# Down projection of a SwiGLU block as seven block products in place of eight, with casts and block sums moved between engines

## The chip, the cores and the metric

One NeuronCore of one Trainium2 chip runs the whole program. The metric is device microseconds for one execution; a kernel's time is the median of several. Six names are used for what works in parallel: TensorE (PE, matmuls; PEld are its loads of the standing operand), VectorE (DVE), ScalarE (ACT), GpSimd (POOL), the 16 DMA engines, and SyncE (SP), whose queue issues nearly all transfers here.

## The reference, cut to what matters

One layer of a latent backbone over 2048 tokens of width 1024. Attention, a gated scan and a Fourier mix come first and are not touched. What the change is about is the end:

```python
x_new = x + g1 * y
x_new = x_new + g2 * swiglu_ffn(modulate(x_new, norm2_g[l], sh2, sc2), w_gate_up[l], w_down[l])
return rms_norm(x_new, final_norm_g)

def swiglu_ffn(h, w_gu, w_dn):
    gate, up = jnp.split(h @ w_gu, 2, axis=-1)
    return (jax.nn.silu(gate) * up) @ w_dn
```

`w_gate_up` is 1024 x 5632 and `w_down` 2816 x 1024, all in float32.

## The kernel before

Every float32 product is made of three matmuls in a 32-bit reduced format (fp32r): an operand `a` is split into a high part (a cast, `hi`) and a low part (`a` minus its cast, `lo`, always on VectorE), and `mm3` adds high x low, high x high and low x high into one PSUM bank. So each operand tile of 128 x 512 costs one cast and one subtraction. The casts of weights (`wparts`) run on GpSimd, those of activations (`split`) on ScalarE.

**Gate-up.** A Strassen-like scheme of seven block products is in use already. The 2048 tokens are two halves `s` of 1024, each two blocks of 512; one unit `(s, j)` works out 128 gate and 128 up features for one half. Its seven products (order 6, 1, 7, 5, 2, 3, 4; 12 matmuls each, 84 a unit, 44 units) gather in three banks, named x, y and z, that are read between products: `act.copy(e6, acc)` after 6, `act.copy(e, acc)` after 1, adds on VectorE after 7, 5, 3 and 4, the gate's SiLU on ScalarE. A bank goes on to its next product when that read is done. Between the products the seven weight operands of the next unit are summed (`left_sums`) and split (`wparts`). The unit's results, `e` and `f`, are the hidden activations of two token blocks; they are stored to DRAM (`hid[b]`). At `s` = 1 new token operands are loaded and split in the last unit of the first half.

**Down.** For each of 4 blocks of 512 tokens and each half of the 1024 output columns, four banks (one per tile of 128 tokens) gather over the 22 tiles of 128 hidden features, in groups of four: `rows` calls `mm3` for every tile. Weights come in pieces of 1024 KB (`wd`, four tiles) and are split for every block anew; hidden tiles are loaded and split once for both column halves. Behind each bank `final` multiplies by the gate `g2`, adds the residual row (`xnew`, loaded again), squares for the norm, and after the second half scales the row tile and stores it: VectorE (L1379, L1380), ScalarE (L1382), GpSimd (L1386, L1387: the power -0.5), then VectorE (L1391) for one half, and ScalarE (L1393) and GpSimd (L1394) for the other.

**Order.** The program is written as one sequence. A planner at build puts each engine's and each queue's instructions into an order, from the written one, the dependencies and its own estimates of durations; an instruction waits on semaphores, and an engine works through its queue in that order. Tiles come from pools with a number of buffers per tag (`wp`: 9 split weights; `h6`, `h1`: 4 each; `wr`: 2 raw pieces); who asks for a buffer waits for the last reader of its old contents.

## Time and profile before

| | us |
|---|---|
| median of 3 runs | 3324.02 |
| lowest, highest | 3322.12, 3328.81 |
| the profiled execution | 3332.05 |
| its span, first to last instruction | 3330.3 |
| TensorE busy in it | 3166.0 |

The rows further down come from the profiled execution, which took 8.0 us more than the median; their times count from the start of its span. Gate-up ends and down begins at 2837.9 us. A row gives an engine's line in the program, the operation, what is written and what is read, and times; a matmul's duration is pipelined, so starts of neighbours, not durations, add up.

### The profile page before, as it was taken

To read this page: it belongs to the slowest core of one execution; us is meant where nothing else is said; L and a number is where in the kernel's file an instruction comes from. 1 tells how busy PE (TensorE), PEld (TensorE's weight loads), DVE (VectorE), ACT (ScalarE), POOL (GpSimd) and SP (SyncE) were. 2 spreads that over 40 slices of the span, in tenths; PEclk is the share of its full clock that TensorE was granted. 3 is DMA by queue.
4 is the path that set the end of the run, shared out by engine and by line. 5 is a ranking of instruction groups with operands and counts; after the bars stand their busy time and mean duration, and the time that the engine had idled before them with its cause. 6 is when DMAs were issued, how large, how long until landed. Compare 5 with 4: busy or idle time off the path is not lost. (4 is left out here: it accounts for less than half of the span.)

```text
span 3330.3 us, 45440 instructions
## 1 busy us (share of the span) xinstructions
PE 3166.0 (95%) x17034; PEld 2649.5 (80%) x17034; DVE 2131.1 (64%) x3211; ACT 952.4 (29%) x2028; POOL 1038.6 (31%) x1241
## 2 busy tenths in 40 slices
PE   7898989999879999999999989999999999999998
PEld 5777777777668888888888767888878888888886
DVE  6575665646776667676666367766776666555543
ACT  3222121222225555555553241111121111212111
POOL 3443452524430121121001443333333333243442
PEclk9999999999989999999999999999999999999999
DMA  6523233143361112120106665422342232664552
GB/s 228 165 70 124 80 104 92 55 117 102 114 186 34 51 49 79 55 69 26 36 32 228 221 218 161 142 76 86 113 134 80 77 95 92 212 211 155 177 171 70
DMA packets 354000, 382.03 MB, mean 115 GB/s; under 512 B 46234, under 2 KB 236532, under 8 KB 352756
## 3 DMA queue, kind: packets, MB, share of 16 engines
q1 hardware_dynamic: 339140, 368.11, 35.2%
q10 hardware_dynamic: 13776, 8.92, 0.8%
q8 instruction: 135, 2.21, 0.3%
q0 software_dynamic: 864, 2.10, 0.2%
q14 instruction: 85, 0.70, 0.1%
HBM read 293.33 MB, written 85.72 MB: 114 GB/s over the span
## 5 line engine op out<-in xcount | busy, mean ns | idle before, releaser
L72 POOL TENSOR_SCALAR wp<-wr 128x512 fp32r<-128x512 f32 x208 | 170.4, 835 | 354.5 <-PE dn L85 234.0
L890 DVE TENSOR_REDUCE mx<-sc 128x1 f32<-128x512 f32 (+1 forms) x320 | 201.9, 632 | 121.9 <-PE sc L888 121.1
L83 PE MATMUL dn<-wp,hdh 128*128 128x512 f32 x704 | 273.9, 389 | 0.0
L84 PE MATMUL dn<-wp,hdh 128*128 128x512 f32 x704 | 273.9, 389 | 0.0
L85 PE MATMUL dn<-wp,hdl 128*128 128x512 f32 x704 | 273.9, 389 | 0.0
L79 DVE TENSOR_TENSOR wp<-wr,wp 128x512 fp32r<-128x512 f32 x208 | 170.8, 859 | 138.9 <-POOL wp L72 138.7
L79 DVE TENSOR_TENSOR ptl<-ptv,pth 128x512 fp32r<-128x512 f32 x288 | 196.4, 686 | 67.3 <-ACT pth L74 65.0
L74 ACT CAST pth<-ptv 128x512 fp32r<-128x512 f32 x288 | 169.7, 593 | 234.1 <-PE ptv L904 223.7
L896 ACT ACTIVATE p<-sc,mx 128x512 f32<-128x512 f32 (+1 forms) x320 | 201.9, 649 | 91.9 <-DVE mx L893 87.7
L83 PE MATMUL y<-xol,wp 128*128 128x512 f32 x528 | 208.7, 395 | 9.8 <-ACT e L1325 4.6
L72 POOL TENSOR_SCALAR wp<-wg 128x512 fp32r<-128x512 f32 x176 | 131.6, 749 | 269.9 <-PE y L85 107.2
L84 PE MATMUL y<-xoh,wp 128*128 128x512 f32 x528 | 206.9, 392 | 0.0
L85 PE MATMUL y<-xoh,wp 128*128 128x512 f32 x528 | 206.6, 392 | 0.0
L79 DVE TENSOR_TENSOR wl<-wraw,wh 128x1536 fp32r<-128x1536 f32 (+3 forms) x78 | 118.7, 1522 | 119.6 <-POOL wh L72 117.0
L85 PE MATMUL accf<-xh,wl 128*128 128x512 f32 x448 | 184.6, 412 | 10.4 <-DVE wl L79 10.4
L888 PE MATMUL sc<-kth,q 128*128 128x512 f32 (+1 forms) x640 | 194.4, 377 | 0.0
L888 PE MATMUL sc<-kp,q 128*128 128x512 f32 (+1 forms) x640 | 190.0, 373 | 0.0
L83 PE MATMUL accf<-xl,wh 128*128 128x512 f32 x448 | 183.9, 410 | 0.4 <-DVE gt L559 0.4
L84 PE MATMUL accf<-xh,wh 128*128 128x512 f32 x448 | 183.1, 409 | 0.0
L79 DVE TENSOR_TENSOR wp<-wg,wp 128x512 fp32r<-128x512 f32 x176 | 128.5, 733 | 84.6 <-POOL wp L72 80.8
L904 PE MATMUL ptv<-ident,p 128*128 128x128 f32 x1152 | 179.1, 275 | 1.8 <-ACT p L896 1.8
L72 POOL TENSOR_SCALAR wp<-ws 128x512 fp32r<-128x512 f32 x132 | 90.2, 683 | 290.0 <-PE z L85 160.8
(367 smaller groups left out, 8426.4 us busy)
## 6 DMA issues: line engine op xcount, KB each, us to landing
wg<-in_w_gate_up_dram SPq DMA_DIRECT2D x88, 512.0 KB, 4.1
wr<-in_w_down_dram SPq DMA_DIRECT2D x40, 1024.0 KB, 5.3
wraw<-in_w_in_dram SPq DMA_DIRECT2D x112, 256.0 KB, 3.7
hr<-hid SPq DMA_DIRECT2D x88, 256.0 KB, 3.1
wm<-in_w_mod_dram SPq DMA_DIRECT2D x64, 256.0 KB, 2.8
hid<-f SPq DMA_DIRECT2D x44, 256.0 KB, 3.0
hid<-e SPq DMA_DIRECT2D x44, 256.0 KB, 2.0
wt<-in_w_mod_dram SPq DMA_DIRECT2D x8, 1024.0 KB, 7.7
```

Of the source, the lines that this page charges most:

```text
L72: pool.tensor_scalar(dst, src, 1.0, 0.0, ALU.mult, ALU.add)
L74: act.copy(dst, src)
L79: (eng or dve).tensor_tensor(dst, src, h, ALU.subtract)
L83: pe.matmul(ps, ah, bl, start=first, stop=False, skip_group_check=more)
L84: pe.matmul(ps, ah, bh, start=False, stop=False, skip_group_check=more)
L85: pe.matmul(ps, al, bh, start=False, stop=last, skip_group_check=more)
L888: pe.matmul(s[:, :n], a[:, ts], bb[:, js], start=i == 0, stop=i == 4)
L890: dve.tensor_reduce(mx[:, j:j + 1], s[:, :n], AX.X, ALU.max)
L896: act.activation(u["p"][:, a:e], u["s"][i][:, :e - a], AF.Exp, bias=mx[:, 5:6], accum_out=mx[:, 6 + i:7 + i])
L904: pe.transpose(pt[:, i, u * P:(u + 1) * P], ps[u]["p"][:, (2 * g + i) * P:(2 * g + i + 1) * P], ident)
```

## The change

The down projection gets the same seven block products. For each token half `s` (two blocks of 512 tokens), the 2816 hidden features are two halves of 11 tiles, the columns two halves of 512. The seven products run in the order 1, 2, 5, 3, 6, 7, 4, each for both token halves at once: eight banks (2 halves x 4 tiles of 128 tokens) gather over 11 steps, taken in groups of two steps and a last one of one. Products 1 and 2 share their banks, so do 5 and 3, and 6, 7 and 4; at the end of each product but the last ScalarE copies the banks out (`drain`), and VectorE, with GpSimd at two places, adds them to the rows during the next product (`rest`, two a group). After product 4 the rows are finished straight from the banks.

The hidden operands of the products (seven, four of them sums, `hidden_sums`) are made on VectorE in gate-up, one sum behind each of four products, and stored: 154 tiles in the place of 88. Units of gate-up come in pairs `(k, k + 11)` to that end, with three buffers for `e` and `f`. The weight operands of products 4 to 7 are differences, made on VectorE from two loaded tiles in down; those of 5 and 6 are stored and used again by 4. All tiles are loaded singly, 256 KB each, two groups ahead (`fetch_down`), and split one group ahead (`split_down`); the first two steps are split in the last unit of gate-up. Each split weight tile now serves all 2048 tokens.

The casts of weights move from GpSimd to ScalarE in gate-up and down (`wparts` has `act` as its default); those of the first unit and of the output projection stay on GpSimd.

```diff
--- before.py
+++ after.py
@@ -65,7 +65,9 @@
     xnew = [dram.tile([TB, D], F32, name=f"xnew{b}") for b in range(NB)]
     x2d = [[dram.tile([512, TB], F32, name=f"x2d{s}{i}") for i in range(4)] for s in range(2)]
     t2d = [[dram.tile([512, TB], F32, name=f"t2d{s}{i}") for i in range(4)] for s in range(2)]
-    hid = [dram.tile([HID, TB], F32, name=f"hid{b}") for b in range(NB)]
+    HH = HT // 2
+    hid = [{n: [dram.tile([P, TB], F32, name=f"hid{s}{n}{k}") for k in range(HH)] for n in range(1, 8)} for s in range(2)]
+    t2w = {n: [dram.tile([P, 512], F32, name=f"t2w{n}{k}") for k in range(HH)] for n in (5, 6)}
 
     def hi(eng, dst, src):
         if eng is pool:
@@ -1060,9 +1062,9 @@
         def raw4(name):
             return wr.tile([P, 4, TB], F32, tag="wr", name=name)
 
-        def wparts(src):
+        def wparts(src, eng=act):
             w = wp.tile([P, 2, TB], F32R, tag="wp", name="wp")
-            hi(pool, w[:, 0, :], src)
+            hi(eng, w[:, 0, :], src)
             lo(w[:, 1, :], src, w[:, 0, :])
             return w
 
@@ -1082,7 +1084,7 @@
             def split(self, i, k):
                 n, k0, nk = self.specs[i]
                 if k < nk:
-                    self.parts.setdefault(i, []).append(wparts(self.raw[i][:, k, :]))
+                    self.parts.setdefault(i, []).append(wparts(self.raw[i][:, k, :], pool))
 
             def split_all(self, i):
                 if i < len(self.specs) and i not in self.done:
@@ -1204,7 +1206,7 @@
                 pt = get()
                 for t in range(4):
                     pe.transpose(pt[:, t * P:(t + 1) * P], xs[k // 4][t][:, k % 4 * P:(k % 4 + 1) * P], ident)
-                xo = ev.tile([P, TB], F32, tag="ef"[k % 2], name="xo")
+                xo = ev.tile([P, TB], F32, tag="ef"[k % 2], bufs=3, name="xo")
                 act.activation(xo, pt, AF.Identity, bias=mod2t[:, k:k + 1], scale=gain2[:, k:k + 1])
                 sp.dma_start(x2d[b // 2][2 * (k // 4) + b % 2][k % 4 * P:(k % 4 + 1) * P, :], xo)
 
@@ -1250,13 +1252,13 @@
                 ks = slice(k * P, (k + 1) * P)
                 mm3(acc, w[:, 0, ks], w[:, 1, ks], x[k][0], x[k][1], first and k == 0, k == 3, not first)
 
-        units = [(s, j) for s in range(2) for j in range(HT)]
+        units = [(s, k + h) for s in range(2) for k in range(HH) for h in (0, HH)]
         raws, ws, xo = [], {}, {}
 
         def first_unit(a, b):
 
             for n in ORDER[a:b]:
-                ws[n] = wparts(raws[-1][n])
+                ws[n] = wparts(raws[-1][n], pool)
 
         def early_sums(ks):
             for k in ks:
@@ -1296,20 +1298,56 @@
         blocks6 = raws.pop()
 
 
-        DG = [(k0, min(4, HT - k0)) for k0 in range(0, HT, 4)]
-        wd = Groups(w_down[0], [(n, k0, nk) for _ in range(NB) for n in range(2) for k0, nk in DG])
-        hidden = []
+        DORDER = (1, 2, 5, 3, 6, 7, 4)
+        DK = [range(k, min(k + 2, HH)) for k in (0, 2, 4, 6, 8)] + [range(10, HH)]
+        steps = [(n, k) for n in DORDER for ks in DK for k in ks]
+        begins = [n * HH + ks[0] for n in range(7) for ks in DK]
+        fetched, ready = {}, {}
         stage = {}
 
-        def more_hidden(upto):
-
-            while len(hidden) < min(upto, NB * HT):
-                i = len(hidden)
-                raw = stage["p"].tile([P, TB], F32, tag="xraw", name="hr")
-                sp.dma_start(raw, hid[i // HT][i % HT * P:(i % HT + 1) * P, :])
-                hidden.append(split(ORDER[i // 4 % 7], "hd", raw))
-
-        stage["p"] = st
+        def fetch_down(i):
+
+            if i >= len(steps) or i in fetched:
+                return
+            n, k = steps[i]
+            if i % 2 == 0:
+                stage["hr"] = raw4("hr")
+            hr = stage["hr"]
+            h = [hr[:, i % 2 * 2 + s, :] for s in range(2)]
+            for s in range(2):
+                sp.dma_start(h[s], hid[s][n][k])
+            w = stage["w"]()
+            at = lambda r, c: w_down[0, (r * HH + k) * P:(r * HH + k + 1) * P, c * 512:(c + 1) * 512]
+            src = {1: [at(0, 0)], 2: [at(1, 0)], 3: [at(1, 1)], 4: [at(1, 0), t2w[6][k]], 5: [at(0, 1), at(0, 0)],
+                   6: [at(1, 1), t2w[5][k]], 7: [at(1, 1), at(0, 1)]}[n]
+            for j, x in enumerate(src):
+                sp.dma_start(w[:, j, :], x)
+            fetched[i] = h, w, len(src)
+
+        def split_down(i):
+            if i >= len(steps) or i in ready:
+                return
+            fetch_down(i)
+            n, k = steps[i]
+            h, w, two = fetched.pop(i)
+            if two == 2:
+                dve.tensor_tensor(w[:, 0, :], w[:, 0, :], w[:, 1, :], ALU.subtract)
+                if n in (5, 6):
+                    sp.dma_start(t2w[n][k], w[:, 0, :])
+            ready[i] = [split((6, 1)[i // 2 % 2], "hd", h[s]) for s in range(2)], wparts(w[:, 0, :])
+
+        stage["w"] = lambda: st.tile([P, 3, 512], F32, tag="ws", name="wd")
+
+        def hidden_sums(s, k, h11, h12, h21, h22):
+
+            t = st.tile([P, 3, TB], F32, tag="ws", name="hs")
+            for q, o, x, y, op in ((5, t[:, 0, :], h21, h22, ALU.add), (6, t[:, 1, :], t[:, 0, :], h11, ALU.subtract),
+                                   (3, t[:, 2, :], h12, t[:, 1, :], ALU.subtract), (7, h21, h11, h21, ALU.subtract)):
+                dve.tensor_tensor(o, x, y, op)
+                sp.dma_start(hid[s][q][k], o)
+                yield
+
+        later = iter(())
         for i, (s, j) in enumerate(units):
             bk = {}
             f32 = lambda tag, bufs: ev.tile([P, TB], F32, tag=tag, bufs=bufs, name=tag)
@@ -1328,11 +1366,11 @@
                         if i + 2 < len(units):
                             raws.append(fetch_w(units[i + 2][1]))
                 elif n == 1:
-                    e = f32("e", 2)
+                    e = f32("e", 3)
                     act.copy(e, acc)
                     pool.tensor_tensor(e6, e6, e, ALU.add)
                 elif n == 7:
-                    f = f32("f", 2)
+                    f = f32("f", 3)
                     dve.tensor_tensor(f, acc, e, ALU.add)
                 elif n == 5:
                     dve.tensor_tensor(f, acc, f, ALU.add)
@@ -1346,74 +1384,134 @@
                     dve.tensor_tensor(e, acc, e, ALU.add)
                     dve.tensor_tensor(e, e, g1, ALU.mult)
                     dve.tensor_tensor(f, f, e6, ALU.mult)
-                    for c, h in enumerate((e, f)):
-                        sp.dma_start(hid[2 * s + c][j * P:(j + 1) * P, :], h)
+                    if j < HH:
+                        sp.dma_start(hid[s][1][j], e)
+                        left = e, f
+                    else:
+                        for q, h in ((2, e), (4, f)):
+                            sp.dma_start(hid[s][q][j - HH], h)
+                        later = hidden_sums(s, j - HH, left[0], e, left[1], f)
+                if o > 0:
+                    next(later, None)
                 if i == 0 and n == 6:
                     xo |= {q: operand(0, q) for q in (2, 3)}
                 if i == 0 and n == 5:
                     turn_rows(NB - 1, xs[NB - 1], range(KT), lambda: bank("pt5"))
                     xo[4] = operand(0, 4)
-                if s == 0 and j == HT - 1:
+                if i + 1 == HT:
                     xo[n] = operand(1, n)
                 if not end:
                     nxt[n] = wparts(blocks6[n])
-                elif o < 3:
-                    more_hidden(4 * (o + 1))
-                    if o == 0:
-                        wd.load(0)
-                        wd.load(1)
-                    for k in ((0, 1), (2,), (3,))[o]:
-                        wd.split(0, k)
-                    wd.done.add(0)
-            if s == 0 and 2 <= j < 6:
-                b11, ts = token_sums(1, j - 2, dve)
-                keep_sums(1, j - 2, ts, range(4))
+                elif o < 2:
+                    split_down(o)
+            if 2 <= i < 6:
+                b11, ts = token_sums(1, i - 2, dve)
+                keep_sums(1, i - 2, ts, range(4))
             ws = nxt
+        for _ in later:
+            pass
         gs.close()
         b1 = ph.enter_context(tc.tile_pool(name="p7b1", bufs=1, reuse_waits="tile"))
-        stage["p"] = ph.enter_context(tc.tile_pool(name="p7s", bufs=3, reuse_waits="tile"))
+        dw = ph.enter_context(tc.tile_pool(name="p7w", bufs=4, reuse_waits="tile"))
+        stage["w"] = lambda: dw.tile([P, 2, 512], F32, tag="dw", name="dw")
         sp.dma_start(fgb, final_norm_g.rearrange("(o n) -> o n", o=1).to_broadcast([P, D]))
 
...
+        rows7 = {}
+        u = [[xpool[4].tile([P, 512], F32, tag=f"{'hl'[s]}4", name="u") for t in range(4)] for s in range(2)]
+        sq = [b1.tile([P, 4, 2], F32, tag="sq7", bufs=4, name="sq7") for _ in range(NB)]
+        halves = [slice(c * 512, (c + 1) * 512) for c in range(2)]
+
+        def load_rows7(a, c):
+            for s in range(2):
+                n = ((5, 7), (2, 3))[s][a]
+                rows7[s, a, c] = [xpool[n].tile([P, 512], F32, tag=f"{'hl'[c]}{n}", name="xs7") for t in range(4)]
+                for t in range(4):
+                    sp.dma_start(rows7[s, a, c][t], xnew[2 * s + a][t * P:(t + 1) * P, halves[c]])
+
+        def square(s, a, c, t):
             junk = b1.tile([P, 512], mybir.dt.bfloat16, tag="junk7", name="junk7")
...
+            act.activation(junk, rows7[s, a, c][t], AF.Square, accum_out=sq[2 * s + a][:, t, c:c + 1])
+
+        def finish_rows(s, a, t):
+            b = 2 * s + a
+            rs = b1.tile([P, 2], F32, tag="rs7", bufs=4, name="rs7")
+            q = sq[b]
+            pool.tensor_scalar(rs[:, 0:1], q[:, t, a:a + 1], 1.0 / D, EPS, ALU.mult, ALU.add)
+            pool.tensor_scalar(rs[:, 1:2], q[:, t, 1 - a:2 - a], 1.0 / D, rs[:, 0:1], ALU.mult, ALU.add)
+            pool.tensor_tensor(rs[:, 0:1], rs[:, 1:2], half[:, 0:1], ALU.pow)
+            for c in range(2):
+                x = rows7[s, a, c][t]
+                if a == 1 and c == 1:
+                    act.activation(x, x, AF.Identity, scale=rs[:, 0:1])
+                elif c == 0 and (a == 0 or t % 2 == 0):
+                    dve.scalar_tensor_tensor(x, x, rs[:, 0:1], fgb[:, halves[c]], ALU.mult, ALU.mult)
+                else:
+                    act.activation(x, x, AF.Identity, scale=rs[:, 0:1])
+                    pool.tensor_tensor(x, x, fgb[:, halves[c]], ALU.mult)
+                sp.dma_start(out[0, b * TB + t * P:b * TB + (t + 1) * P, halves[c]], x)
+
+        def tmp():
+            return b1.tile([P, 512], F32, tag="tmp7", bufs=8, name="tmp7")
+
+        def gated(eng, x, y, c):
+            eng.tensor_tensor(y, y, g2b[:, halves[c]], ALU.mult)
+            eng.tensor_tensor(x, x, y, ALU.add)
+
+        rest = []
+
+        def drain(n, s, t, acc):
+
+            if n == 4:
+                x = rows7[s, 1, 0][t]
+                dve.tensor_tensor(acc, acc, g2b[:, halves[0]], ALU.mult)
+                dve.tensor_tensor(x, acc, x, ALU.add)
+                square(s, 1, 0, t)
+                finish_rows(s, 1, t)
                 return
...
+            y = u[s][t] if n == 1 else tmp()
+            act.copy(y, acc)
+            if n > 1:
+                rest.append(lambda: add_product(n, s, t, y))
+
+        def add_product(n, s, t, y):
+            if n in (5, 3):
+                dve.tensor_tensor(y, y, u[s][t], ALU.add)
+                gated(dve, rows7[s, int(n == 5), 1][t], y, 1)
+                if n == 3:
+                    gated(pool, rows7[s, 1, 0][t], u[s][t], 0)
+            else:
+                a, c = {2: (0, 0), 6: (0, 1), 7: (1, 1)}[n]
+                x = rows7[s, a, c][t]
+                gated(dve, x, y, c)
+                square(s, a, c, t)
+                if n == 6:
+                    finish_rows(s, a, t)
+                elif n == 7:
+                    pool.tensor_tensor(x, x, fgb[:, halves[1]], ALU.mult)
+
+        for g, i in enumerate(begins):
+            n, ks = DORDER[g // len(DK)], DK[g % len(DK)]
+            if ks[0] == 0 and n in (1, 5, 6):
+                acc = [[bank("dn") for t in range(4)] for s in range(2)]
+            after = (begins + [len(steps)] * 3)[g + 1:g + 4]
+            for q in range(after[0], after[1]):
+                split_down(q)
+            for q in range(after[1], after[2]):
+                fetch_down(q)
+            for _ in range(2):
+                if rest:
+                    rest.pop(0)()
+            if n == 1 and ks[0] in (2, 4, 6, 8):
+                load_rows7(*{2: (0, 0), 4: (1, 1), 6: (0, 1), 8: (1, 0)}[ks[0]])
+            ops = [ready.pop(i + q) for q in range(len(ks))]
             for s in range(2):
...
                 for t in range(4):
...
+                    ts = slice(t * P, (t + 1) * P)
+                    for k, (h, w) in zip(ks, ops):
+                        mm3(acc[s][t], h[s][0][:, ts], h[s][1][:, ts], w[:, 0, :], w[:, 1, :],
+                            n in (1, 5, 6) and k == 0, k == HH - 1, n not in (1, 5, 6))
+                    if ks[-1] == HH - 1:
+                        drain(n, s, t, acc[s][t])
 
 
 _INS = ['x', 'c', 'ctx', 'c_ctx', 'w_mod', 'b_mod', 'norm1_g', 'norm2_g', 'w_in', 'q_norm_g', 'w_uq', 'kv_norm_g',
```

## Rows read from the trace of the kernel before

**Rows 1.** The page: span and busy time of each engine (share, instructions).
```profile
span 3330.3 us, 45440 instructions
...
PE 3166.0 (95%) x17034; PEld 2649.5 (80%) x17034; DVE 2131.1 (64%) x3211; ACT 952.4 (29%) x2028; POOL 1038.6 (31%) x1241
```

**Rows 2.** Busy time by stretch: stretch, length, engines (x count), PE clock, DMA share, GB/s.
```profile
2600.00:2820.00 220.00, 220.00 (x972) 182.18 (x971) 142.49 (x192) 27.96 (x47) 68.52 (x92) 1.00 0.28 85
...
2838.00:2860.00 22.00, 22.00 (x99) 18.22 (x98) 12.57 (x18) 6.74 (x11) 5.81 (x8) 1.00 0.72 254
...
1860.00:1890.00 30.00, 30.00 (x139) 24.98 (x139) 9.87 (x16) 12.15 (x24) 9.32 (x12) 0.91 0.79 279
...
2838.00:3317.00 479.00, 478.81 (x2113) 396.14 (x2111) 252.24 (x326) 79.76 (x153) 173.82 (x223) 1.00 0.50 166
```

**Rows 3.** Instructions of the down sums' tile: durations in ns, first and last start.
```profile
L83 PE MATMUL dn<-wp,hdh x704: 389/389/389, 2837.9 to 3316.0; 128*128 128x512 f32 x176
...
L85 PE MATMUL dn<-wp,hdl x704: 388/389/389, 2838.4 to 3316.4; 128*128 128x512 f32 x176
```

**Rows 4.** Waits of TensorE from 2000 to 2838 us: total, times, longest.
```profile
PE y L83 <- ACT e L1325: 4.6, 2, 2.9
```

**Rows 5.** Groups of instructions from 2838 to 3317 us: busy us, mean ns, idle before.
```profile
L72 POOL TENSOR_SCALAR wp<-wr 128x512 fp32r<-128x512 f32 x168 | 140.4, 850 | 246.8 <-PE dn L85 234.0 <-DMA wr<-in_w_down_dram 7.0 <-issue 1.8
...
L79 DVE TENSOR_TENSOR hdl<-hr,hdh 128x512 fp32r<-128x512 f32 x81 | 69.9, 885 | 87.9 <-ACT hdh L74 73.9 <-PE dn L84 13.9
L74 ACT CAST hdh<-hr 128x512 fp32r<-128x512 f32 x80 | 49.7, 621 | 144.9 <-PE dn L84 81.3 <-DMA hr<-hid 61.5
...
L1382 ACT ACTIVATE junk<-xt 128x512 bf16<-128x512 f32 x30 | 18.8, 628 | 235.5 <-DVE xt L1380 227.8 <-ACT junk L1382 4.4 <-issue 3.2
```

**Rows 6.** The same view of a quiet stretch of gate-up, 2100 to 2300 us.
```profile
L79 DVE TENSOR_TENSOR wp<-ws,wp 128x512 fp32r<-128x512 f32 x32 | 33.3, 1040 | 6.7 <-POOL wp L72 5.4
...
L1325 ACT COPY e<-y 128x512 f32<-128x512 f32 x11 | 6.5, 589 | 43.6 <-PE y L85 43.6
```

**Rows 7.** Transfers of the down stage: total, then by issue, KB, us to landing.
```profile
DMA packets 39205, 79.33 MB, mean 166 GB/s; under 512 B 2670, under 2 KB 2670, under 8 KB 39178
...
wr<-in_w_down_dram SPq DMA_DIRECT2D x36, 1024.0 KB, 5.3
hr<-hid SPq DMA_DIRECT2D x79, 256.0 KB, 3.0
```

**Rows 8.** Timeline of VectorE at the end: start, duration, instruction [idle before].
```profile
3312.77 0.70 DVE L1379 TENSOR_TENSOR dn<-dn,g2b 128x512 f32<-128x512 f32 x1 [12.88 <-PE dn L85]
...
3314.13 0.70 DVE L1379 TENSOR_TENSOR dn<-dn,g2b 128x512 f32<-128x512 f32 x1
3314.86 0.69 DVE L1380 TENSOR_TENSOR xt<-dn,xt 128x512 f32<-128x512 f32 x1
3316.04 0.75 DVE L1391 SCALAR_TENSOR_TENSOR xt<-xt,rs,g1b 128x512 f32<-128x512 f32 x1 [0.49 <-POOL rs L1387]
```

**Rows 9.** Timeline of GpSimd at the end.
```profile
3315.11 0.27 POOL L1386 TENSOR_SCALAR rs<-sq,rs 128x1 f32<-128x1 f32 x1 [15.95 <-ACT junk L1382]
3315.46 0.55 POOL L1387 TENSOR_TENSOR rs<-rs,half 128x1 f32<-128x1 f32 x1
...
3318.10 0.26 POOL L1386 TENSOR_SCALAR rs<-sq,rs 128x1 f32<-128x1 f32 x1
...
3325.94 1.26 POOL L1394 TENSOR_TENSOR xt<-xt,g1b 128x512 f32<-128x512 f32 x1 [0.83 <-ACT xt L1393]
```

**Rows 10.** Timeline of VectorE where gate-up ends.
```profile
2834.66 0.69 DVE L79 TENSOR_TENSOR wp<-wr,wp 128x512 fp32r<-128x512 f32 x1
2835.26 0.69 DVE L79 TENSOR_TENSOR hdl<-hr,hdh 128x512 fp32r<-128x512 f32 x1
...
2841.45 0.68 DVE L1347 TENSOR_TENSOR e<-e,g 128x512 f32<-128x512 f32 x1
```

More of the change, by code (lines that the diff above doesn't have):

```diff
@@ L1375, in tile_backbone @@
         sp.dma_start(fgb, final_norm_g.rearrange("(o n) -> o n", o=1).to_broadcast([P, D]))
-        def final(b, t, c, acc, xs, sq, rs):
-            ns = slice(c * 512, (c + 1) * 512)
-            dve.tensor_tensor(acc, acc, g2b[:, ns], ALU.mult)
-            dve.tensor_tensor(xs[t][:, ns], acc, xs[t][:, ns], ALU.add)
-            junk = b1.tile([P, 512], mybir.dt.bfloat16, tag="junk7", name="junk7")
-            act.activation(junk, xs[t][:, ns], AF.Square, accum_out=sq[:, t, c:c + 1])
-            if c == 0:
-                pool.tensor_scalar(rs[:, t, 0:1], sq[:, t, 0:1], 1.0 / D, EPS, ALU.mult, ALU.add)
-                return
-            pool.tensor_scalar(rs[:, t, 1:2], sq[:, t, 1:2], 1.0 / D, rs[:, t, 0:1], ALU.mult, ALU.add)
-            pool.tensor_tensor(rs[:, t, 0:1], rs[:, t, 1:2], half[:, 0:1], ALU.pow)
-            for s in range(2):
-                ns = slice(s * 512, (s + 1) * 512)
-                if s == 0:
-                    dve.scalar_tensor_tensor(xs[t][:, ns], xs[t][:, ns], rs[:, t, 0:1], fgb[:, ns], ALU.mult, ALU.mult)
-                else:
-                    act.activation(xs[t][:, ns], xs[t][:, ns], AF.Identity, scale=rs[:, t, 0:1])
-                    pool.tensor_tensor(xs[t][:, ns], xs[t][:, ns], fgb[:, ns], ALU.mult)
-                sp.dma_start(out[0, b * TB + t * P:b * TB + (t + 1) * P, ns], xs[t][:, ns])
@@ L1397, in tile_backbone @@
-        for b in range(NB):
-            sq = b1.tile([P, 4, 2], F32, tag="sq7", bufs=2, name="sq7")
-            rs = b1.tile([P, 4, 2], F32, tag="rs7", bufs=2, name="rs7")
-            for c in range(2):
-                acc = [bank("dn") for _ in range(4)]
-                for g, (k0, nk) in enumerate(DG):
-                    i = (b * 2 + c) * len(DG) + g
-                    wd.ahead(i + 1)
-                    more_hidden(b * HT + (min(4 * g + 12, HT) if c == 0 else HT))
-                    if c == 0 and g == 2:
-                        xs = [b1.tile([P, D], F32, tag="xt7", bufs=4, name="xt7") for t in range(4)]
-                        for t in range(4):
-                            sp.dma_start(xs[t], xnew[b][t * P:(t + 1) * P, :])
-                    w = wd.parts.pop(i)
-                    for t in range(4):
-                        rows(acc[t], t, hidden[b * HT:], w, k0, nk, HT)
-                    if c == 1:
-                        more_hidden((b + 1) * HT + min(4 * g + 10, HT))
-                for t in range(4):
-                    final(b, t, c, acc[t], xs, sq, rs)
+        rows7 = {}
```

## The prediction, made before the kernel was changed

> **What bounds the kernel now.** I read the page first, its busy times and its 40 slices. TensorE is busy 3166 of 3330 us; VectorE, the next, 2131 [rows 1]. That share is an average, so I asked each stage for itself. In a quiet stretch of gate-up (2600 to 2820 us) and in the whole down stage (2838 to 3317 us) TensorE is busy all the time at a granted clock of 1.00, the upper of its two levels, 2.4 GHz, while VectorE has a third to a half of its time free and ScalarE and GpSimd most of it [rows 2]. Then the tile of the down sums: its first matmul starts at 2837.9 us, its last at 3316.4, 3 x 704 of them [rows 3]. That is (3316.4 - 2837.9) / 2111 = 0.2267 us from start to start without a gap; the 389 ns of a row are pipelined, and 0.2267 is what one matmul costs the path. So in down the count of matmuls sets the time. TensorE's own waits after 2000 us are short and sit in gate-up's first units and where it changes the token half, the longest group 4.6 us in all [rows 4]. Last comes the tail: after the last matmul (ends 3316.8) four row tiles are still scaled and stored, until 3330.3: 13.5 us [rows 1, 3].
>
> **The matmuls.** Down now takes 4 blocks of tokens x 4 row tiles x 2 column halves x 22 x 3 = 2112 matmuls. Seven products instead of eight half-size ones, for each of two token pairs, take 2 x 7 x 4 x 11 x 3 = 1848, of the same shape, with the same operand standing. Saved: 264 x 0.2267 = 59.8 us, if nothing else sets the pace. Gate-up keeps its matmuls.
>
> **The work beside them in down.** VectorE: low parts for 154 hidden tiles (88 before) and 77 weight tiles (176 before), 44 weight sums, and at the ends of products some 124 passes (16, 24, 24, 24, 16 and 20 for products 2, 5, 3, 6, 7 and 4, two or three for each of 8 banks): 399 against about 360 before. A pass is 0.69 us uncontended, and its successor starts after 0.60 [rows 10]; the low parts of hidden tiles, with GpSimd beside them, average 0.885 [rows 5]. So 240 to 353 us in a stage of 1848 x 0.2267 = 419: not the bound. ScalarE: 231 casts x 0.62, 48 copies x 0.59, and 32 squares and 20 scalings x 0.63 [rows 5, 6], 204 us of 419. GpSimd loses its 168 casts of 0.85 us. What can cost is order: operands for a group of two steps (48 matmuls, 10.9 us) need slots that come free with the group before last, so their split must fit into one group. Split of two steps: 6 low parts, up to 2 sums; with the two rests of an earlier product, up to 14 passes, 9.7 us at 0.69 and 12.4 at 0.885. Where the latter holds, four groups overrun by 1.5 us each, and the last two groups of the product, which carry no rests, take it back. The rests of product 6 are worse if they run as written: VectorE scales a tile only after ScalarE's square and GpSimd's root, some 2 us idle twice a group, three or four groups long, up to 10 us. The trace speaks against written order: at the end VectorE runs L1379 and L1380 of a second row tile before L1391 of the first [rows 8], so other work is put into such waits. I take 2 us, bounds 0 and 10.
>
> **The seam.** Today the seam has no gap, since the first groups are split in the last unit. After the change two steps (10.9 us of TensorE) are split there, until 2837.9 + 10.9 = 2848.8 on the old axis. The weights of the third and fourth step go into a pool that takes the place of gate-up's, so their loads wait behind its last users. Now VectorE ends the unit's last product at 2842.1 [rows 10]; then come four new sums (2.4 us), a store and a load (3.0 each, as a load lands [rows 7]), a cast and a low part (1.3): 2851.8. Those two steps are thus 3 us late, the second of them somewhat more. Beside it, four groups of product 1 also load 2.1 MB of rows each: with 1.6 MB of operands, 3.7 MB per 10.9 us, 337 GB/s, where the best stretch shows 279 at a DMA share of 0.79 [rows 2]. Each such group falls 2 us behind, and the lead of one group covers it nearly. I take 5 us for both, bounds 0 (the memory is free early) and 12 (one of those loads stands behind the 2.1 MB of rows, 7.5 us at 279 GB/s).
>
> **The tail.** Now four row tiles are left over, at 3.0 us each: GpSimd sits in a chain of L1386, L1387, ScalarE, L1394, whose starts stand 3.0 apart, and starts 2.3 us after the first drain at 3312.8 [rows 8, 9]. After the change all eight banks end within the last 24 matmuls (5.4 us), the first 4.8 us before the last. Even tiles need of GpSimd three small passes (0.9 + 0.35 = 1.25 us), odd ones the 3.0 us chain and one small pass (3.35). Four pairs are 18.4 us: -4.8 + 2.3 + 18.4 + 3.1 (last pass to end, 3327.2 to 3330.3 [rows 1, 9]) = 19 after the last matmul, against 13.5: 6 us more. In written order, with each tile's scaling ahead of the next tile's drain, a pair takes, from the even tile's square on, 0.8 (square) + 0.95 (root) + 0.75 (scaling) + 1.4 (the odd tile's drain) + 0.8 + 0.95 + 2 x 0.72 (ScalarE's scalings) = 7.1 us, and the tail grows by 15; with VectorE's 16 x 0.70 + 4 x 0.75 = 14.2 us as the only limit, and 4 us of chain behind, it grows by 3. Bounds 3 and 15.
>
> **Gate-up.** Casts of weights move from GpSimd to ScalarE: 7 x 0.62 = 4.3 us a unit (19.0 us of TensorE) on an engine that is 13% busy [rows 2, 5]. They now queue between copies that TensorE needs: y's copy must end within product 1, 12 x 0.2267 = 2.7 us; with one cast ahead of it, it takes 0.62 + 0.59 = 1.2 [rows 5, 6], 1.5 us short of that. If that cover went, product 7 would be late, then all of the unit. VectorE gets two sums a unit more (1.4 us) and loses contention: a low part beside GpSimd averages 1.04 us, against the 0.69 of a free one [rows 6, 10]. Sixty-six more stores of 256 KB ride on 85 GB/s [rows 2]. At the two places where TensorE waits, ScalarE's extra casts and VectorE's shorter passes pull against each other. I take 1 us more, bounds -5 and +6. The deeper buffers and the new order of units cost nothing that a row shows: a unit's work is the same.
>
> **Transfers, and a rule against the change.** Down moves 362 transfers, nearly all of 256 KB, where weights came in pieces of 1024 KB: 95 MB in 419 us, 227 GB/s, against 79 MB at 166 [rows 7]. One 256 KB load lands 3.0 us after issue, one of 1024 KB 5.3 [rows 7]: one at a time that would be 87 GB/s. But 22 us of the stage show 254 GB/s at a share of 0.72 [rows 2], so loads overlap, and I charge nothing beyond the seam's 5 us. The Trainium skill (DMA: Bandwidth & Descriptors, Bandwidth) says to batch transfers to 1 MiB or more for three quarters of the peak; by the fit on that page (its section on the anatomy of one DMA, for GpSimd's path) a 256 KB transfer would take an estimated 2.6 us. One after another the 362 would by that page take an estimated 940 us in the place of 479, and the sum would be some +460 us in the place of the -46 below; the trace does not agree, since two or more are in flight at 254 GB/s.
>
> **Sum**, on the profiled execution's own 3332.05 us: -59.8 + 5 + 2 + 6 + 1 = -46, so 3286. That execution is 8.0 us above the median of the runs, 3324.02; so 3278.
>
> **Rivals.**
> 1. *Written order*: the chains through ScalarE and GpSimd hold VectorE and TensorE. -59.8 + 9 (seam) + 10 + 15 + 4 = -22: 3302. For it: the planner's view of a chain may be short. Against it: the order in [rows 8]. 0.22.
> 2. *Everything is covered*: seam and stage at 0, tail +3, gate-up -3: -60, 3264. For it: VectorE loses its contention. 0.09.
> 3. *Transfers set the pace of down* (other side): each group waits for its own loads, at the place where a fetch needs slots freed two groups earlier. At 185 GB/s 95 MB take 515 us; with the tail's 6 and the seam's 5, against 479: +47, 3371. It decides from where the stage takes 479 - 12 = 467 us: below 204 GB/s the kernel is slower. For it: the stage has shown no more than 166 on average [rows 7]. Against it: it asked for no more, at a share of 0.50, and 254 and 279 were reached [rows 2]. 0.07. The Trainium skill's rule on batching (DMA: Bandwidth & Descriptors, Bandwidth) points this way.
> 4. *No change to measure*: y's copy comes late by 1.0 us in each of gate-up's 44 units, with more than two casts ahead of it, and eats the gain. For it: such a wait has been seen [rows 4]. Against it: twice in 44 units. 0.03.
>
> The forecast, with 3262 to 3294 as its own range, has 0.59. A difference of 0.2% (7 us) is about what a measurement of this kernel can tell. Faster: 0.59 + 0.22 + 0.09 = 0.90; same 0.03; slower 0.07. The range goes from rival 2 less 4 us to rival 1 with a few us of late loads more: 3260 to 3308.
>
> **What the profile will show.** Right: 1848 down matmuls, 0.227 us apart, 419 to 426 us from first to last, a gap of a few us some 11 us after the first; 17 to 21 us after the last matmul; gate-up's time within a few us of now; low parts near 0.69 us. Wrong: gaps between groups ended by DMA (rival 3) or by low parts after a wait on the root (rival 1); product 7 of gate-up waiting for y's copy in every unit; a granted clock below 1.00 in down.

## The result, and the profile after

| | before | after |
|---|---|---|
| median, both in alternation on one chip | 3325.65 (4 runs) | 3286.9 (4 runs, 3281.53 to 3292.29) |
| the profiled execution (its span) | 3332.05 (3330.3) | 3281.53 (3279.7) |

The ratio is 0.988, with a 95% interval of 0.9867 to 0.9893: 36 to 44 us faster. 3278 was forecast; the measured time lies 9 us above it, inside the range of 3260 to 3308. The four runs after lie in two pairs, 3281.53 and 3283.52, 3290.28 and 3292.29, and the profile below is that of the fastest.

The page of the kernel after, against [rows 1]: TensorE has 264 matmuls fewer and 64 us less to do, VectorE as much as before, ScalarE 269 us more, GpSimd 249 less.

```profile
span 3279.7 us, 45162 instructions
...
PE 3101.9 (95%) x16770; PEld 2594.1 (79%) x16770; DVE 2135.6 (65%) x3354; ACT 1221.2 (37%) x2524; POOL 789.4 (24%) x784
```

The tile of the down sums after, against [rows 3], with what TensorE waited for:

```profile
L85 PE MATMUL dn<-wp,hdh x616: 387/389/796, 2820.1 to 3257.5; 128*128 128x512 f32 x154
...
L87 PE MATMUL dn<-wp,hdl x616: 387/389/795, 2820.5 to 3257.9; 128*128 128x512 f32 x154
...
  ACT tmp L1472: 5.2, 2
  DVE hdl L81: 5.0, 7
  DVE wp L81: 1.2, 1
```

1848 matmuls, as announced, but in 3258.3 - 2820.1 = 438.2 us, not 419 to 426: 1848 x 0.2267 is 418.9, so 19.3 us are lost. The maximum of 796 ns, twice the median, points at a lower clock, which the rows below show. Stage by stage, in the profiled executions:

| us | before | after | difference |
|---|---|---|---|
| up to gate-up's first y matmul | 1975.1 | 1958.8 | -16.3 |
| from there to the first down matmul | 862.8 | 861.3 | -1.5 |
| first to end of last down matmul | 478.9 | 438.2 | -40.7 |
| from there to the end of the span | 13.5 | 21.4 | +7.9 |

The first row is not the change's doing: the order of instructions there is the same on every engine, and over the twelve profiles that have this part as it is after the change (most of the experiments below) it takes from 1958.8 to 1974.5 us, and 1969.7 in e5, which has the kernel before's. The other rows sum to -34, the medians give -39.

Busy time by stretch, columns as in [rows 2]. First gate-up's quiet stretch and all of down; then down in three parts: most of products 1 to 6, the 90 us around product 7, and the rest:

```profile
2582.00:2802.00 220.00, 220.00 (x973) 182.21 (x972) 144.37 (x220) 73.92 (x128) 24.58 (x11) 1.00 0.34 109
2820.00:3258.00 438.00, 426.57 (x1850) 348.83 (x1848) 268.26 (x381) 171.75 (x330) 110.35 (x64) 0.99 0.58 196
...
2820.00:3112.00 292.00, 290.77 (x1283) 240.49 (x1282) 178.31 (x258) 114.76 (x213) 58.79 (x20) 1.00 0.65 219
3112.00:3202.00 90.00, 79.79 (x321) 62.08 (x320) 58.43 (x83) 38.35 (x76) 25.60 (x28) 0.94 0.58 198
3202.00:3258.00 56.00, 56.00 (x249) 46.27 (x247) 31.52 (x41) 18.64 (x41) 25.97 (x16) 1.00 0.21 68
```

Nearly all of the loss is in one place: 90 us have room for 397 matmuls, and 321 ran. 76 x 0.2267 = 17 us: 10 idle, and 7 in the busy time, where the granted clock averages 0.94. Ten microseconds of it:

```profile
3150.00:3160.00 10.00, 7.36 (x24) 4.96 (x24) 8.48 (x12) 4.48 (x10) 5.56 (x7) 0.83 0.56 191
```

TensorE's timeline inside them shows where the clock goes. After 2.37 us without work the next matmuls start 0.42 to 0.43 us apart where nothing else holds them, at the lower level of 1.2 GHz, until 3156.95; then 0.23 again. The seven from 3153.39 on take 3.56 us in the place of 1.59. Of the 2.0 us more the clock has 7 x 0.2 = 1.4, another wait for VectorE the rest:

```profile
3150.62 0.40 PE L86 MATMUL dn<-wp,hdh 128*128 128x512 f32 x1
3153.39 0.62 PE L87 MATMUL dn<-wp,hdl 128*128 128x512 f32 x1 [2.37 <-DVE hdl L81]
3153.81 0.63 PE L85 MATMUL dn<-wp,hdh 128*128 128x512 f32 x1
...
3156.95 0.43 PE L85 MATMUL dn<-wp,hdh 128*128 128x512 f32 x1
3157.22 0.39 PE L86 MATMUL dn<-wp,hdh 128*128 128x512 f32 x1
```

The idle time ends with a low part of VectorE. What makes VectorE late begins a product earlier (`e2_sums_vector` below tests this), in GpSimd's timeline (start, duration):

```profile
3059.80 23.24 POOL L1457 TENSOR_TENSOR u<-u,g2b 128x512 f32<-128x512 f32 x1 [107.33 <-DVE tmp L1478]
3083.11 1.70 POOL L1458 TENSOR_TENSOR xs<-xs,u 128x512 f32<-128x512 f32 x1
3084.76 1.74 POOL L1457 TENSOR_TENSOR u<-u,g2b 128x512 f32<-128x512 f32 x1
```

and in VectorE's over the same time:

```profile
3080.60 1.28 DVE L1334 TENSOR_TENSOR dw<-dw 128x512 f32<-128x512 f32 x2
3082.96 0.69 DVE L1334 TENSOR_TENSOR dw<-dw 128x512 f32<-128x512 f32 x1 [1.08 <-DMA dw<-in_w_down_dram]
3083.57 1.78 DVE L81 TENSOR_TENSOR hdl<-hr,hdh 128x512 fp32r<-128x512 f32 x1
3085.28 1.78 DVE L81 TENSOR_TENSOR wp<-dw,wp 128x512 fp32r<-128x512 f32 x1
```

One GpSimd pass takes 23 us while VectorE runs without a pause, and ends when VectorE first stands still (3081.9 to 3083.0). From then on the two alternate, and each VectorE pass with two operands takes 1.78 us in the place of 0.69, up to 3108. The Trainium skill (SBUF — State Buffer, Who interferes with whom) says that VectorE and GpSimd share one pair of ports as an exclusive lock; the trace agrees, with 1.78 beside 0.69. On average over down the low parts of hidden tiles take 804 ns, between the 690 announced and the 885 of [rows 5]:

```profile
L81 DVE TENSOR_TENSOR hdl<-hr,hdh 128x512 fp32r<-128x512 f32 x146 | 116.0, 804 | 84.5 <-ACT hdh L76 50.6 <-PE dn L86 32.6 <-PE dn L87 1.3
```

### The profile page after: what moved, and what is told of

Read it like the earlier page. It is cut to its first block, busy times and chain, and to the rows that moved or that the text cites. A ratio compares the mean times of both kernels' runs of the same rounds, so it can differ in the third digit from the quotient of the medians.

```text
span 3279.7 us, 45162 instructions
## 1 busy us (share of the span) xinstructions
PE 3101.9 (95%) x16770; PEld 2594.1 (79%) x16770; DVE 2135.6 (65%) x3354; ACT 1221.2 (37%) x2524; POOL 789.4 (24%) x784
## 4 chain that ended last, share of the span: by engine, by line
PE 53%; DMA 4%; DVE 3%; POOL 2%; ACT 1%; issue 1%; SPq 0%; POOLq 0%; DVEq 0%; ACTq 0%
PE sc L890 7%; PE dn L85 3%; PE dn L87 3%; PE dn L86 3%; PE y L87 3%; PE y L85 3%; PE y L86 3%; PE ptv L906 3%; PE z L85 2%; PE z L87 2%; PE z L86 2%; PE x L86 2%; PE x L87 2%; PE x L85 2%; PE po L87 1%; PE po L86 1%
## 5 line engine op out<-in xcount | busy, mean ns | idle before, releaser
L1371 POOL TENSOR_TENSOR e<-e,e 128x512 f32<-128x512 f32 x44 | 91.3, 2076 | 751.1 <-ACT e L1370 689.6
L85 PE MATMUL dn<-wp,hdh 128*128 128x512 f32 x616 | 241.9, 393 | 6.4 <-ACT tmp L1472 5.2
L87 PE MATMUL dn<-wp,hdl 128*128 128x512 f32 x616 | 242.2, 393 | 5.0 <-DVE hdl L81 5.0
L86 PE MATMUL dn<-wp,hdh 128*128 128x512 f32 x616 | 241.4, 392 | 0.0
L81 DVE TENSOR_TENSOR hdl<-hr,hdh 128x512 fp32r<-128x512 f32 x154 | 121.8, 803 | 84.9 <-ACT hdh L76 50.9
L85 PE MATMUL po<-ptl,ckh 128*128 128x256 f32 x576 | 169.1, 294 | 0.0
L76 ACT CAST hdh<-hr 128x512 fp32r<-128x512 f32 x154 | 94.4, 621 | 188.8 <-PE dn L86 145.0
```

What stands on the lines that cost most here:

```text
L76: act.copy(dst, src)
L81: (eng or dve).tensor_tensor(dst, src, h, ALU.subtract)
L85: pe.matmul(ps, ah, bl, start=first, stop=False, skip_group_check=more)
L86: pe.matmul(ps, ah, bh, start=False, stop=False, skip_group_check=more)
L87: pe.matmul(ps, al, bh, start=False, stop=last, skip_group_check=more)
L1371: pool.tensor_tensor(e6, e6, e, ALU.add)
```

## The experiments

All times are medians; ratios are to the kernel before, run on the same chip. "Down" is first to end of last down matmul of the profiled run.

**Is it SyncE's queue?** In product 7 the stores of finished rows wait at the head of SyncE's queue, with loads behind them:

```profile
3134.16 18.94 SPq L1451 DMA_DIRECT2D out_dram<-xs  x10
3153.36 1.78 SPq L1318 DMA_DIRECT2D hr<-hid  x4
```

`e1_late_stores` holds the stores of product 6's rows back until the last hidden tile is loaded; `e1b_traffic` does too, and issues stores of the same size, of a ready tile, where the real ones would have been, so that the traffic stays.

```diff
-                sp.dma_start(out[0, b * TB + t * P:b * TB + (t + 1) * P, halves[c]], x)
+                put = lambda x=x, c=c: sp.dma_start(out[0, b * TB + t * P:b * TB + (t + 1) * P, halves[c]], x)
+                if a == 0:
+                    held.append(put)
+                else:
+                    put()
...
+            if after[1] == len(steps):
+                with tc.issue_after(stage["last"]):
+                    while held:
+                        held.pop(0)()
```

> The sixteen stores of the rows finished in product 7 are queued behind the last operand load; all computing stays where it was. Queue theory (loads of operands stand behind stores that wait for the finishing chain, and come late): the down stage, first to last matmul, falls from 438 us to 421 to 425, the time by 13 to 17 us against the changed kernel (3287 to about 3272), and the dips of the granted clock in product 7 go. Chain theory (VectorE itself is late, since it works in order through waits on ScalarE and GpSimd): the stage stays at 434 to 438 and the time within 4 us. Traffic theory (the stores' bytes take the transfers' time): gains like the queue theory.

> As the run with late stores, but at the old place of each late store, in product 7, stands a store of 256 KB of data that is always ready, into a buffer nobody reads: the same bytes at the same time, no wait. Queue theory: as with late stores, within 3 us of it. Traffic theory: the gain is gone, within 4 us of the changed kernel.

Measured: 3292.25, ratio 0.989 (0.9875 to 0.9904), and 3294.71, 0.9898 (0.9882 to 0.9915); down 443.8 and 444.3. No gain, from the queue or from the traffic. But these two profiles differ from that of the changed kernel in more than the stores: GpSimd's first pass of product 6 takes 1.58 us in them, not 23.24, VectorE's long passes begin that much sooner, and TensorE loses 3 us in product 6 already.

```profile
3065.91 1.58 POOL L1461 TENSOR_TENSOR u<-u,g2b 128x512 f32<-128x512 f32 x1 [106.34 <-DVE tmp L1482]
```

So the queue is judged by the next experiment, which leaves the stores where they were, and by `e12_late_stores2`, which has this edit without GpSimd's sums.

**Are they GpSimd's sums?** `e2_sums_vector` gives GpSimd's 24 full passes of the sums (16 in product 6, 8 in product 4) to VectorE.

```diff
-                    gated(pool, rows7[s, 1, 0][t], u[s][t], 0)
+                    gated(dve, rows7[s, 1, 0][t], u[s][t], 0)
...
-                    pool.tensor_tensor(x, x, fgb[:, halves[1]], ALU.mult)
+                    dve.tensor_tensor(x, x, fgb[:, halves[1]], ALU.mult)
```

> GpSimd's 16 passes in product 6 and 8 in product 4 go to VectorE; the finishing chain of product 7 keeps its GpSimd steps. Chain theory: VectorE's passes in product 6 fall from 1.78 us to 0.69, it enters product 7 early, the stage is 5 to 10 us shorter. Queue theory: VectorE had its lateness covered in product 6 (TensorE has no gap there), product 7 waits as before: stage 436 to 440, time within 3 us.

Measured: 3276.66, ratio 0.9843 (0.9829 to 0.9858), so by the ratios 12 us below the changed kernel; down 427.3. More work on the busier engine, and it is done sooner. For this gain two rivals fall. The stores stand as long at the head of SyncE's queue as before, and in the 90 us around product 7 VectorE waits as long for the root as in the changed kernel (the second row is the same in both):

```profile
3129.38 18.96 SPq L1451 DMA_DIRECT2D out_dram<-xs  x10
...
DVE xs L1447 <- POOL rs L1441: 7.4, 8, 2.5
```

What differs is when VectorE gets there: its first scaling of product 7 starts 302.7 us after down's first matmul, in the changed kernel 311.5. How much the 24 passes cost varies: down takes 434.1 to 444.3 us in the four profiles with them (the changed kernel, e1, e1b, e4), 427.3 to 428.4 in the four without (e2, e6, e7, e12). What is left, some 8 us, stands at the change from product 7 to product 4.

**The casts.** `e3_casts_gpsimd` gives the casts of weights back to GpSimd in the changed kernel; `e5_casts_alone` moves those of gate-up's units to ScalarE in the kernel before.

```diff
-        def wparts(src, eng=act):
+        def wparts(src, eng=pool):
```

> The changed kernel with the casts of weights given back to GpSimd in gate-up and down (the default of wparts is pool again); all else as changed. Contention theory (GpSimd's passes and VectorE's two-input passes shut each other out, and the stretches where VectorE runs without a pause are where TensorE loses time): 77 casts of about 0.85 us come back on GpSimd in down, and in the stretches of sums each of them can wait for a pause of VectorE, so groups are late: down 445 to 465 us instead of 438, kernel 3293 to 3315, low parts of weights back above 0.85 us. ScalarE-queue theory (casts and bank copies wait behind one another on ScalarE, and GpSimd does no harm): ScalarE loses 77 casts in down, its copies come sooner, down 428 to 438 us, kernel 3276 to 3287.

> The kernel before with one part of the change alone: the casts of weights in gate-up's units go to ScalarE (first unit, output projection and down stay on GpSimd). Theory that gate-up is bound by TensorE's matmuls wherever the casts run: VectorE's low parts fall from 1.04 to about 0.70 us, and the time stays within 3 us of before: ratio 0.999 to 1.001. Rival, y's copy queued behind casts on ScalarE: one more us in many of 44 units, ratio 1.003 to 1.013. Rival, VectorE's contention costs gate-up time now: ratio 0.997 to 0.999.

Measured: e3 3354.85, ratio 1.0078 (1.0064 to 1.0092), slower than before; e5 3316.77, ratio 0.9964 (0.9952 to 0.9976), a little beyond what its second rival gave. TensorE's 4.6 us for y's copy [rows 4] are no longer among its waits in e5; that contention was behind them is argued, not shown. In e3 down takes 460.7, inside what contention gave, but the kernel is 40 us above its range: gate-up, of which the expectation said nothing, loses more. TensorE's waits of e3 in gate-up, then the quiet stretch:

```profile
PE z L85 <- DVE f L1376: 27.4, 18, 3.4
...
2580.00:2800.00 220.00, 213.01 (x936) 175.07 (x935) 157.44 (x210) 27.01 (x45) 76.78 (x90) 1.00 0.32 100
```

VectorE is at 157 of 220 us with GpSimd at 77, where e5 has 136 and 15, and TensorE waits for VectorE's adds to the banks. So gate-up is known in all four corners, from its first y matmul to down's first:

| gate-up, us | casts on GpSimd | casts on ScalarE |
|---|---|---|
| without the hidden sums | 862.8 (before) | 856.4 (e5) |
| with them | 902.8 (e3) | 861.3 (after) |

The hidden sums (with the new order of units) cost 40 us beside GpSimd's casts and 5 without; the move of the casts is worth 6 or 41. The ten other profiles with the gate-up of the changed kernel have 857.9 to 861.5 us, so the 5 may be as little as 1.5. Neither has a price without the other.

**The tail.** `e4_wide_end` takes the last three steps of product 4 as one group, so that the last banks end further apart.

```diff
+        DL = DK[:4] + [range(8, HH)]
+        groups = [(n, ks) for n in DORDER for ks in (DL if n == 4 else DK)]
+        begins = [DORDER.index(n) * HH + ks[0] for n, ks in groups]
...
-            ready[i] = [split((6, 1)[i // 2 % 2], "hd", h[s]) for s in range(2)], wparts(w[:, 0, :])
+            ready[i] = [split(4 if i + 1 == len(steps) else (6, 1)[i // 2 % 2], "hd", h[s]) for s in range(2)], wparts(w[:, 0, :])
```

> The last product's groups are 2, 2, 2, 2, 3 steps in the place of 2, 2, 2, 2, 2, 1, so that the eight banks end 9 x 0.2267 = 2.04 us apart and not 0.68; the last step's hidden tiles take buffers of their own. Pile theory (eight drains stand behind the last matmuls): the tail after the last matmul falls from 21.4 us to 12 to 15, the time by 6 to 9 us. Rival (the group of three waits at its start for operands that one group of lead used to cover, and gives the gain back): the tail falls alike, but a gap of 5 us or more opens before the last group, time within 2 us.

Measured: 3289.54, ratio 0.987 (0.984 to 0.99), not to be told from the changed kernel by its time; in the profile (of an execution of 3271.13 us) the tail is 16.1 us in the place of 21.4, somewhat less of a gain than was expected, and no gap of 5 us opens before the last group. With e2's edit it repeats (`e6_sums_wide`):

> The two experiments that helped, together: GpSimd's 24 full passes of products 6 and 4 on VectorE, and the last group of product 4 with three steps in the place of two and one, so that the last banks end further apart. If the two are independent, down as in the first of them (427 us) and the tail as in the second (16 us instead of 21): kernel 3269 to 3273, ratio to before 0.982 to 0.984. If the tail's gain is taken back by a later start of the last group (three steps of operands in one split): 3275 to 3280, as with the sums alone.

Measured: 3273.22, ratio 0.9835 (0.9822 to 0.9849); down 427.6, tail 16.0: the two are independent in the profile, though between e6 and e2 the intervals overlap.

**What is left at product 7.** `e7_sums_hr3` is e2 with a third pair of buffers for hidden tiles, taken from the split weights' nine.

```diff
+            if i // 2 % 3 == 2:
+                hr = wp.tile([P, 2, TB], F32, tag="wp", name="hr")
+                h = [hr[:, s, :] for s in range(2)]
```

> The sums on VectorE as before, and beside it every third pair of steps loads its hidden tiles into two buffers of the split weights, so that three pairs instead of two are in flight. With the sums on VectorE one stall of some 4 to 6 us (with the clock's fall behind it) was left at the change from product 7 to 4, where ScalarE stood 6.9 us for a load of hidden tiles with the copies of the banks behind it. Theory that the loads come late because their buffer came free late: the stall goes, down 420 to 424 us, kernel 3269 to 3273. Rival, the loads are late because the whole chain of casts, low parts and squares is late there: no change, 3275 to 3279.

Measured: 3278.73, ratio 0.984 (0.9826 to 0.9855), down 428.4: no change, so a third pair got in this way does not help. Three edits on top of e6: `e9_scale_vector` takes GpSimd's last full passes, the eight multiplies that finish product 6's rows, to VectorE, and the eight scalings ahead of them on ScalarE go with them; `e10_late_finish` asks for those finishes a row tile later; `e11_both` has both.

```diff
-                elif c == 0 and (a == 0 or t % 2 == 0):
+                elif a == 0 or t % 2 == 0:
```

```diff
+                stage.pop("fin", int)()
                 if n == 6:
-                    finish_rows(s, a, t)
+                    stage["fin"] = lambda: finish_rows(s, a, t)
```

> The sums on VectorE and the wide last group, and beside them the last of GpSimd's full passes ahead of the tail: the second column half of product 6's rows is scaled in one pass on VectorE in the place of one on ScalarE and one on GpSimd (8 row tiles). What is left of the loss in down stands at the change from product 7 to product 4, some 5 to 7 us. Contention theory: in product 7 VectorE's passes lengthened beside these eight of GpSimd, so its operands came late at the product's end; the stall goes, down 420 to 424 us in the place of 427, kernel 3266 to 3270, ratio 0.981 to 0.983. Rival, the chain square, root, scaling holds VectorE's queue there whoever does the scaling: no change, ratio 0.983 to 0.985.

> The sums on VectorE and the wide last group, and the finish of product 6's rows (root and scaling) asked for one row tile later in the written order, so that VectorE has a tile's sums to do while ScalarE's square and GpSimd's root run. Chain theory: VectorE's waits on the root (8 us in all in product 7) go, with them the stall at the change to product 4: down 420 to 424 us, ratio 0.981 to 0.983. Contention theory: GpSimd's eight multiplies stay, so the stall stays: ratio 0.983 to 0.985.

> Both edits of the two runs before this one. If either theory alone is right it is as fast as that one, 3266 to 3270; if each holds half of the stall, this alone reaches down 420 to 422 us and a ratio of 0.980 to 0.982; if the stall is of neither, 0.983 to 0.985.

Measured: e9 3266.57, ratio 0.9826 (0.9811 to 0.984), down 420.3; e10 3270.16, 0.983 (0.9815 to 0.9845), down 425.2; e11 3262.51, 0.9818 (0.9804 to 0.9831), down 420.4. The intervals overlap; the stage tells them apart. The same 90 us of e6, then of e9:

```profile
3121.00:3211.00 90.00, 85.56 (x368) 69.79 (x367) 64.11 (x92) 43.96 (x90) 28.86 (x32) 0.98 0.60 207
```

```profile
3128.00:3218.00 90.00, 90.00 (x399) 74.53 (x398) 71.55 (x116) 43.72 (x94) 14.38 (x24) 1.00 0.64 215
```

321 matmuls in the changed kernel, 368 without GpSimd's sums, 399, all that fit, without its multiplies, while VectorE's busy time grows from 58 to 64 to 72 us. In e9 the low parts take 686 ns (710 in e6) and VectorE waits 7.5 us for the root (10.4 in e6, 8.8 in e10, by the same view; so e10 hardly took away the waits that it was made for):

```profile
L81 DVE TENSOR_TENSOR hdl<-hr,hdh 128x512 fp32r<-128x512 f32 x146 | 98.2, 686 | 82.7 <-ACT hdh L76 52.5 <-PE dn L86 28.9 <-DMA hr<-hid 1.3
...
L1449 DVE SCALAR_TENSOR_TENSOR xs<-xs,rs,g1b 128x512 f32<-128x512 f32 x18 | 12.9, 748 | 7.5 <-POOL rs L1443 7.5
```

e9 takes more than GpSimd's multiplies away. In e6 the eight scalings wait for the root in ScalarE's queue, with casts behind them; in e9 this row is gone:

```profile
ACT xs L1451 <- POOL rs L1443: 11.1, 7, 3.0
```

e9 also lets the stores of those rows go sooner. `e12_late_stores2` tests that reading: e6 with e1's edit, the multiplies left on GpSimd.

> The sums on VectorE and the wide last group, and the stores of product 6's finished rows issued only after the last loads of hidden tiles, so that no load of product 7 or 4 stands behind a store on SyncE's queue. GpSimd's eight multiplies (second column half of product 6's rows) stay. Two readings of the run that moved these multiplies to VectorE and lost the stall at the change to product 4. Contention: the multiplies lengthened VectorE's passes; then the stall stays here, down 425 to 428 us, ratio 0.983 to 0.985. Queue: the multiplies made the rows late, their stores waited at the head of SyncE's queue, up to 19 us, and the loads behind them were late; then the stall goes here too, down 420 to 423 us, ratio 0.981 to 0.983.

Measured: 3273.89, ratio 0.9829 (0.9816 to 0.9843); down 427.6 as in e6, with the same stall, 3.5 us for ScalarE's copy of a bank and a clock of 0.83 behind it:

```profile
3190.00:3200.00 10.00, 6.54 (x22) 4.92 (x21) 4.75 (x9) 6.12 (x12) 0.00 (x0) 0.83 0.60 205
```

The queue falls again, now with GpSimd's sums out of the way: on the stage's 427.6 us, since the interval of the ratio alone holds both readings. What is left for e9's 7 us is VectorE's passes beside the eight multiplies, VectorE's waits for the root and ScalarE's; no run parts them.

## Why the prediction came out as it did

- **Matmuls, -59.8**: right. 1848, 0.227 us apart wherever they ran undisturbed (e9's stage is 420.3, 1.4 us over 418.9).
- **Seam, +5**: mis-sized. TensorE waits 1.2 us for the third step's weights and starts again 1.4 us late (first row below). The 2 us a group charged for 337 GB/s were not due: the first stretch shows 336 GB/s at a DMA share of 0.98, and TensorE has no gap there, nor from 2850 to 2860 us, at 333 GB/s and 0.99:

```profile
2832.36 0.50 PE L85 MATMUL dn<-wp,hdh 128*128 128x512 f32 x1 [1.23 <-DVE wp L81]
...
2820.00:2830.00 10.00, 10.00 (x46) 8.29 (x45) 4.83 (x8) 1.24 (x2) 0.00 (x0) 1.00 0.98 336
```

- **Order in down, +2 (bounds 0 to 10)**: the step that failed, with some 18 us in its place, above its upper bound. The working priced contention as an average, 0.885 us a low part, taken from rows in which GpSimd ran casts; GpSimd's own new passes were counted nowhere. They raise a pass to 1.78 us, so that VectorE comes to product 7 some 9 us late (e2: 11 us of down), and there it has no slack. The bound of 10 was put on VectorE's waits for the root. They are there, but the same 7.4 us in e2, where TensorE waits only 1.1 us for low parts in these 90 us, against 5.0. Of the 7 us more that e9 gains, a part is 2.9 us less of such waits, since GpSimd's multiply also stood ahead of the next root, and a part may be ScalarE's eight scalings; the cause of these 7 stays open among the three. And 17 us lost are only 10 us idle: the fall of the clock after idle stretches had no term in the sum.
- **Tail, +6**: +7.9 measured; 19 us were forecast after the last matmul, 21.4 came. Pairs follow each other by 4.6, 5.7 and 3.3 us, about the 4.6 of the working; in it VectorE waits for the root, as in these two of four:

```profile
3261.99 0.75 DVE L1447 SCALAR_TENSOR_TENSOR xs<-xs,rs,g1b 128x512 f32<-128x512 f32 x1 [1.43 <-POOL rs L1441]
...
3267.72 0.75 DVE L1447 SCALAR_TENSOR_TENSOR xs<-xs,rs,g1b 128x512 f32<-128x512 f32 x1 [2.59 <-POOL rs L1441]
```

- **Gate-up, +1**: -1.5 measured, a sum of -6.4 and +5 (e5, and after against e5), -1 to -5 over all profiles with this gate-up. That the two "pull against each other" was right; that they depend on one another, 40 us, was not seen.
- **Rivals.** Written order (3302) is right in part: VectorE does hold TensorE in product 7, but the waits in its queue alone cost little (e2); it takes the lateness from product 6 as well. Transfers as the pace (3371) is out: 85.7 MB at 196 GB/s in a stage whose loss has other causes, against 79 MB [rows 7]:

```profile
DMA packets 46910, 85.69 MB, mean 196 GB/s; under 512 B 5217, under 2 KB 5217, under 8 KB 46882
```

  Everything covered (3264) is about what e9 and e11 reach. No wait for y's copy is left among TensorE's in gate-up, where before it was the longest [rows 4].

The sum was off by +16 - 3.6 + 2 - 2.5 = +12 us in the profiled executions, and by 9 in the medians. That it stayed in the range is in part luck: seam and gate-up gave back 6 of the 16 us that the order in down had cost beyond its term.

## What to carry to other kernels

A pass with two SBUF operands that is moved to an idle GpSimd is not free while VectorE runs such passes: price it as a VectorE pass of 1.78 us in the place of 0.69, in the stretch where it runs, not over the stage. Before an engine is relieved, ask what it shares with the one that takes the work: here 24 passes more on the busier engine gave 11 us of down back. And when an edit takes one pass away, look what else goes with it on the other engines: e9's 7 us have three possible owners. Change two things that meet on such a resource in all four combinations; here the same move was worth 6 us in one kernel and 41 in the other.

## What the runs showed of the hardware that was not expected

A GpSimd pass with two operands, about 1.7 us when it alternates, stood 23.24 us while VectorE ran such passes without a pause (23.25 in e4's profile). That is not a rule: in e1 and e1b the same pass, begun at the same place in VectorE's work and again with no pause of VectorE, was through in 1.58 us. VectorE's rows around its start, in the changed kernel and in e1:

```profile
3058.93 1.29 DVE L1478 TENSOR_TENSOR tmp<-tmp,u 128x512 f32<-128x512 f32 x2
3060.14 0.68 DVE L81 TENSOR_TENSOR hdl<-hr,hdh 128x512 fp32r<-128x512 f32 x1
```

```profile
3065.05 1.29 DVE L1482 TENSOR_TENSOR tmp<-tmp,u 128x512 f32<-128x512 f32 x2
3066.25 1.78 DVE L81 TENSOR_TENSOR hdl<-hr,hdh 128x512 fp32r<-128x512 f32 x1
```

What decides which of the two gets its turn no run shows. Where GpSimd got it at once, down took 443.8 and 444.3 us, against 438.2 and 434.1. Once GpSimd has its turn, the two engines alternate, and VectorE, which lost nothing before, pays 1.1 us for each pass that meets one of GpSimd's. And a wait of 2.37 us cost TensorE some 1.4 us more, since the seven matmuls behind it ran at the lower clock.
